# mLSTM chunk products in a hybrid backbone on one Trainium2 core: state products and scores alternate between partition halves

## The chip, the cores and the metric

The kernel runs on one core of a Trainium2 chip. Times are device microseconds of one launch, from the runs of the whole program. A core has TensorE (matmuls, with a loader of weights that overlaps them; PE and PEld in the profile), VectorE (DVE), ScalarE (ACT), GpSimd (POOL) and SyncE (SP, which here only issues DMAs). Matmul results go to PSUM, which the program uses in banks of 128 partitions by 512 fp32 values.

## The reference

A two-layer backbone over 256 context and 256 latent tokens of width 1024. Each layer is half a SwiGLU feed-forward, a token mixer, half a SwiGLU feed-forward. The mixer of layer 0 is a bidirectional mLSTM (8 heads, key width 64, value width 128, chunks of 128 tokens), that of layer 1 a retention. What matters here is one chunk of the mLSTM, for one head and direction:

```
s   = (q k^T) * exp(d - m_t)                          # 128 x 128, masked
num = w_inter * (q C) + s v                           # 128 x 128
den = w_inter * (q n) + sum(s)
h   = num / max(|den|, exp(-m_t))
C, n = w_prev * (C, n) + k^T (w_s * v), w_prev * n + k^T w_s
```

`C` is the state that the chunks before left (64 x 128), `n` its normaliser. The first context chunk of each direction has no state yet.

## The kernel before, in words

Everything lies on one core. Large matmuls are made from three products of split fp32r parts (`mm3`, lines 151 to 153), with weights streamed from memory, split by ScalarE and VectorE (lines 147 and 148) and used once. TensorE, ScalarE, VectorE and GpSimd each run their instructions in the order in which a scheduler, with its own simulated times, has put them; under `in_order()` TensorE's instructions keep the order in which they are written.

The mLSTM is done for two groups of four heads (`hh` 0 and 1). Of a group's four heads, two pairs `i` and in each pair `g` = 0 or 1: head `g` has its 64 key channels on partitions 0 to 63 or 64 to 127 of `q` and `k`. `ktok` transposes the keys, `states` computes the states of both directions for the chunks (line 738; its outputs alternate between partition halves), and `intra(s, hh)` computes the outputs of segment `s` (0 context, 1 latent), which has two chunks `c`, in two directions `d`. So there are four calls of `intra`, each with four chunks of four heads. `n` is a chunk's place in its direction; where `n` is 0 there is no state.

`intra` first makes the scores (line 761): for each half `g` one PSUM bank with four products of 64 x 128 by 64 x 128. For each direction it loads a broadcast of the row maxima (`E`, tile `b4`, L769, by GpSimd) and of the state weights (`WI`, L772), masks `E` (GpSimd, L776), takes exponentials (ScalarE, L779), multiplies them by the scores (VectorE, L782) and weights `q` (L783). Then for each chunk and each half `g` a bank gets, for the two pairs, `E` times the values (L794, contracting over 128 tokens) and `WI` times the state (L797, contracting over the half's 64 channels), the two taking turns in one accumulation. Column 128 is the denominator: ScalarE takes its magnitude (L800), VectorE bounds and inverts it (L801, L802), and the outputs are scaled into `hs` by ScalarE in direction 0 (L806) and added by VectorE in direction 1 (L808). `fin` normalises `hs` over the head, multiplies by the gate (GpSimd, L833) and transposes it (TensorE, L836) for the output projection.

All banks named `A` come from one pool of four; scores, chunk outputs and transposes share it. The calls stand among projections: the values and gates (`vo`, banks `Y`) beside the two calls of `hh` 0, then the states of `hh` 1, `intra(0, 1)`, the first output products, and `intra(1, 1)`, which is chained in written order with the next output products (`wout`).

Of the kernel before, what the change touches and what calls it, by code (L numbers as in the profile page):

```python
# [17 lines left out]
AF = mybir.ActivationFunctionType  # L18
# [69 lines left out]
def build(nc, tc, dr, out):  # L88
    V, S, G, TE = nc.vector, nc.scalar, nc.gpsimd, nc.tensor
# [15 lines left out]
    def bankA():  # L105
        return psA.tile([128, 512], F32, name="A", tag="A")
# [4 lines left out]
    def t2k(dtype=F32, n=512):  # L111
        return tmp.tile([128, 520], dtype, name="t", tag="t")[:, :n]

    def in_order():

        return tc.manual_schedule(engines={mybir.EngineType.PE})

    def seg(s):
        return slice(s * 256, s * 256 + 256)
# [345 lines left out]
    def mlstm(on_tile, on_seg):  # L465
# [138 lines left out]
        def chain(*f):  # L604

            def fn(W):
# [4 lines left out]
            return (fn,) + f[-1][1:]  # L611

        res += [part(ktok, 0), part(states, 0), part(intra, 0, 0)] + v1 + [part(intra, 1, 0)] + v2
        res += [part(ktok, 1)] + v3[:1] + [part(states, 1)] + v3[1:]
        res += [part(fin, 0, 0), part(intra, 0, 1), part(fin, 1, 0), wout(0, 0), chain(part(intra, 1, 1), wout(0, 1)), part(fin, 0, 1),
                part(fin, 1, 1), wout(1, 0), wout(1, 1)]
        res.append((lambda W: st.close(), None, None))
# [132 lines left out]
    def intra(X, s, hh):  # L750

        q, k, v = X["q"], X["k"], X["v"][hh]
        ti = [slice(s * 256 + c * 128, s * 256 + c * 128 + 128) for c in range(2)]
        sb = []
        for g in range(2):
            ps = bankA()
            o = g * 64
            for i in range(2):
                for c in range(2):
                    x = (i * 2 + c) * 128  # L760
                    TE.matmul(ps[:, x:x + 128], k[o:o + 64, hh * 2 + i, ti[c]], q[o:o + 64, hh * 2 + i, ti[c]],
                              start=True, stop=True)
            sb.append(ps.rearrange("p (i t) -> p i t", i=2))
        hs = X["p2"].tile([128, 2, 4, 128], F32, name="hs", tag="hs")
        X["hs"][s, hh] = hs
        for d in range(2):
            r0 = d * 32 + s * 16 + hh * 8
            E = X["p2"].tile([128, 8, 128], F32, name="b4", tag="b4")
            nc.gpsimd.dma_start(out=E, in_=X["nwd"][0][r0:r0 + 8].partition_broadcast(128))  # L769
            WI = t2k().rearrange("p (i t) -> p i t", i=2)  # L770
            for g in range(2):
                nc.gpsimd.dma_start(  # L772
                    out=WI[g * 64:g * 64 + 64],
                    in_=X["nwd"][1][r0:r0 + 8].rearrange("(i g c) t -> g i (c t)", g=2, c=2)[g].partition_broadcast(64))
            sg = 1 - 2 * d
            G.affine_select(out=E, in_=E, pattern=[[0, 8], [sg, 128]], base=0, channel_multiplier=-sg,  # L776
                            compare_op=ALU.is_ge, fill=NEG)
            for x in range(8):
                S.activation(out=E[:, x], in_=E[:, x], func=AF.Exp, bias=X["a"][:, r0 + x:r0 + x + 1])  # L779
            Ev = E.rearrange("p (i g c) t -> p g i (c t)", i=2, g=2)  # L780
            for g in range(2):
                V.scalar_tensor_tensor(out=Ev[:, g], in0=sb[g], scalar=0.125, in1=Ev[:, g], op0=ALU.mult, op1=ALU.mult)  # L782
            V.scalar_tensor_tensor(out=WI, in0=q[:, hh * 2:hh * 2 + 2, seg(s)], scalar=0.125, in1=WI,  # L783
                                   op0=ALU.mult, op1=ALU.mult)
            emv = X["em"][:, r0:r0 + 8].rearrange("p (i g c) -> p g c i", i=2, g=2)
            for c in range(2):
                n = s * 2 + (c ^ d)
                hv = hs[:, c].rearrange("p (i g) e -> p g i e", g=2)
                for g in range(2):
                    o = g * 64  # L790
                    ps = bankA()[:, :258].rearrange("p (i e) -> p i e", i=2)
                    with in_order():
                        for i in range(2):
                            TE.matmul(ps[:, i, :], E[:, i * 4 + g * 2 + c], v[:, s * 2 + c, 2 * i + g, :],  # L794
                                      start=True, stop=(n == 0))
                            if n:
                                TE.matmul(ps[:, i, :], WI[o:o + 64, i, c * 128:c * 128 + 128], X["C", d, n - 1][o:o + 64, i],  # L797
                                          start=False, stop=True)
                    dn = small.tile([128, 2], F32, name="dn")
                    S.activation(out=dn, in_=ps[:, :, 128], func=AF.Abs)  # L800
                    V.tensor_tensor(out=dn, in0=dn, in1=emv[:, g, c], op=ALU.max)  # L801
                    V.reciprocal(out=dn, in_=dn)  # L802
                    hg = hv[:, g]
                    for i in range(2):
                        if d == 0:
                            S.activation(out=hg[:, i, :], in_=ps[:, i, 0:128], func=AF.Copy, scale=dn[:, i:i + 1])  # L806
                        else:
                            V.scalar_tensor_tensor(out=hg[:, i, :], in0=ps[:, i, 0:128], scalar=dn[:, i:i + 1],  # L808
                                                   in1=hg[:, i, :], op0=ALU.mult, op1=ALU.add)

    def fin(X, s, hh):
# [498 lines left out]
    for i, (fn, src, mode) in enumerate(steps):  # L1310
# [3 lines left out]
        n = wi[i]  # L1314
# [14 lines left out]
```

## Time and profile before

| | |
|---|---|
| median of 3 runs | 1918.21 us (1915.36 to 1919.32) |
| the profiled execution | 1913.94 us, span 1912.1 us |
| TensorE busy | 1878.6 us (98%) |
| VectorE, ScalarE, GpSimd busy | 62%, 36%, 9% |
| DMA | 147 GB/s mean |
| mean granted TensorE clock | 0.991 |

The span runs from the first to the last instruction; the rest of the execution's time lies around it. The mLSTM's chunks are in 500 to 640 us of the span. The profile gives for each matmul a record with its start and a modelled end, so that neighbouring records overlap; how long an instruction holds the engine is read from the start of one to the start of the next. A product of two fp32 operands has two records. A form such as 64\*128 is the part of the array that an instruction uses: rows (the contraction) by columns. A release behind an arrow is what ended the idle time ahead of a row.

### The profile page before, as it was taken

What the parts mean: (1) busy time and instruction counts of PE and PEld (TensorE: products, weight loads), DVE (VectorE), ACT (ScalarE), POOL (GpSimd) and SP (SyncE); (2) the same over time, 40 slices, a digit from 0 to 9 for tenths busy, and PEclk for the clock granted to TensorE, in tenths of its full rate; (3) what the DMA queues carried; (4) which work ended last, traced back from release to release, by engine and by line L of the source; (5) the groups of instructions that cost most, each with busy time, mean ns of one, the idle gap of its engine ahead of it and who ended that gap; (6) DMA issues with size and microseconds to landing.
All of it is one profiled execution on the core that took longest, in us unless ns stands there. A gap on an engine that the chain in (4) does not pass through costs nothing.

```text
span 1912.1 us, 25440 instructions
## 1 busy us (share of the span) xinstructions
PE 1878.6 (98%) x10142; PEld 1617.0 (85%) x10142; DVE 1192.0 (62%) x1965; ACT 696.8 (36%) x1061; POOL 167.2 (9%) x207
## 2 busy tenths in 40 slices
PE   8999999999999999999999999999999999999998
PEld 6888888887777898888888988888898888889998
DVE  6858878566866566677764655555466555565554
ACT  4432232243553352222333422223244444444443
POOL 3000000110132210000001000000112120110001
PEclk9999999999998999999999999999999999989999
DMA  8536656223323234455542344554334244235652
GB/s 315 194 125 209 209 176 206 91 86 99 102 94 100 100 100 139 148 198 176 187 176 89 111 145 167 187 195 165 116 105 129 98 138 132 99 123 170 205 177 89
DMA packets 171689, 280.58 MB, mean 147 GB/s; under 512 B 6210, under 2 KB 108738, under 8 KB 171186
## 3 DMA queue, kind: packets, MB, share of 16 engines
q1 hardware_dynamic: 168656, 268.59, 42.0%
q0 software_dynamic: 2912, 10.36, 1.7%
q8 instruction: 80, 1.31, 0.3%
q14 instruction: 39, 0.31, 0.0%
q10 hardware_dynamic: 2, 0.01, 0.0%
HBM read 277.82 MB, written 1.11 MB: 146 GB/s over the span
## 4 chain that ended last, share of the span: by engine, by line
PE 91%; DVE 4%; ACT 2%; DMA 1%; issue 1%; POOL 1%; SPq 0%; POOLq 0%; DVEq 0%; ACTq 0%
PE A L152 18%; PE A L151 18%; PE A L153 18%; PE Y L152 11%; PE Y L151 11%; PE Y L153 11%; PE A L794 1%; PE A L797 1%; PE Y L1095 1%; DVE wl L148 1%; DMA XT<-xt 0%; DMA t<-nwd 0%; ACT wh L147 0%; DVE XT L210 0%; DVE so L551 0%
## 5 line engine op out<-in xcount | busy, mean ns | idle before, releaser
L148 DVE TENSOR_TENSOR wl<-raw,wh 128x1024 fp32r<-128x1024 f32 x360 | 448.0, 1245 | 465.9 <-ACT wh L147 465.6
L147 ACT ACTIVATE wh<-raw 128x1024 fp32r<-128x1024 f32 x360 | 382.2, 1062 | 808.1 <-PE A L152 324.7
L152 PE MATMUL A<-xl,wh 128*128 128x512 f32 (+1 forms) x1712 | 599.5, 352 | 6.8 <-DVE xl L148 6.1
L153 PE MATMUL A<-xh,wl 128*128 128x512 f32 (+1 forms) x1712 | 598.2, 351 | 0.0
L151 PE MATMUL A<-xh,wh 128*128 128x512 f32 (+1 forms) x1712 | 592.4, 352 | 5.6 <-ACT xh L1112 2.6
L152 PEld LDWEIGHTS A<-xl,wh 128*128 128x128 f32 x1712 | 325.8, 190 | 51.0 <-DVE xl L148 7.6
L151 PEld LDWEIGHTS A<-xh,wh 128*128 128x128 f32 x1712 | 321.5, 191 | 48.9 <-ACT xh L1112 2.9
L153 PEld LDWEIGHTS A<-xh,wl 128*128 128x128 f32 x1712 | 325.8, 190 | 42.4
L247 DVE CUSTOM_DVE_ANT_0 mj<-mr,mc,VT 128x1024 bf16<-128x1024 f32 x224 | 287.0, 1281 | 4.7 <-DMA mr<-mod_t 1.9
L153 PE MATMUL Y<-gh,wl 128*128 128x512 f32 (+1 forms) x704 | 246.0, 350 | 0.0
L151 PE MATMUL Y<-gh,wh 128*128 128x512 f32 (+1 forms) x704 | 245.5, 350 | 0.0
L152 PE MATMUL Y<-gl,wh 128*128 128x512 f32 (+1 forms) x704 | 245.3, 349 | 0.0
L153 PEld LDWEIGHTS Y<-gh,wl 128*128 128x128 f32 x704 | 132.3, 188 | 18.5
L152 PEld LDWEIGHTS Y<-gl,wh 128*128 128x128 f32 x704 | 132.4, 188 | 18.2
L151 PEld LDWEIGHTS Y<-gh,wh 128*128 128x128 f32 x704 | 132.3, 188 | 17.5
L152 PE MATMUL Y<-wl,xh 128*128 128x512 f32 x320 | 126.2, 395 | 0.0
L151 PE MATMUL Y<-wh,xh 128*128 128x512 f32 x320 | 125.3, 393 | 0.0
L153 PE MATMUL Y<-wh,xl 128*128 128x512 f32 x320 | 125.0, 392 | 0.0
L173 POOL TENSOR_TENSOR nacc<-nacc,nsq 128x256 f32<-128x256 f32 x50 | 41.6, 840 | 644.8 <-ACT nsq L169 643.4
L147 ACT ACTIVATE gh<-s 128x512 fp32r<-128x512 f32 (+1 forms) x88 | 48.7, 568 | 84.9 <-DVE s L338 84.9
L210 DVE SCALAR_TENSOR_TENSOR XT<-Y,GT,XT 128x256 f32<-128x256 f32 x148 | 63.8, 477 | 21.3 <-PE Y L153 21.1
L338 DVE TENSOR_TENSOR s<-s,A 128x512 f32<-128x512 f32 (+1 forms) x88 | 54.3, 619 | 28.5 <-PE A L153 28.2
(269 smaller groups left out, 1826.2 us busy)
## 6 DMA issues: line engine op xcount, KB each, us to landing
raw<-w SPq DMA_DIRECT2D x126, 1024.0 KB, 5.2
mr<-mod_t SPq DMA_DIRECT2D x128, 512.0 KB, 3.9
raw<-r_in SPq DMA_DIRECT2D x24, 1024.0 KB, 5.2
raw<-m_in SPq DMA_DIRECT2D x12, 1024.0 KB, 5.3
raw<-r_out SPq DMA_DIRECT2D x8, 1024.0 KB, 5.6
raw<-w SPq DMA_DIRECT2D x12, 512.0 KB, 3.7
w<-mod_t SPq DMA_DIRECT2D x8, 512.0 KB, 10.7
w<-mod_s SPq DMA_DIRECT2D x8, 512.0 KB, 10.6
```

The costliest lines, as they stand in the source:

```text
L147: S.activation(out=hi, in_=src, func=AF.Copy)
L148: return V.tensor_tensor(out=lo, in0=src, in1=hi.bitcast(F32), op=ALU.subtract)
L151: TE.matmul(ps, l[0], r[0], start=first, stop=False)
L152: TE.matmul(ps, l[0], r[1], start=False, stop=False)
L153: return TE.matmul(ps, l[1], r[0], start=False, stop=last)
L173: G.tensor_tensor(out=N[s][0], in0=N[s][0], in1=sq, op=ALU.add)
L210: V.scalar_tensor_tensor(out=XT[:, k, seg(s)], in0=ps, scalar=gate[:, s, k:k + 1], in1=XT[:, k, seg(s)], op0=ALU.mult, op1=ALU.add)
L247: V.tensor_tensor_reduce(out=mp["j"], in0=raw[i], in1=mp["c"][:, w], scale=1.0, scalar=MB[:, l * 72 + f:l * 72 + f + 1], op0=ALU.mult, op1 ...
L338: V.tensor_tensor(out=g[:, a:z], in0=sv[m][:, a:z], in1=ps[m][:, a:z], op=ALU.mult)
L794: TE.matmul(ps[:, i, :], E[:, i * 4 + g * 2 + c], v[:, s * 2 + c, 2 * i + g, :], start=True, stop=(n == 0))
L797: TE.matmul(ps[:, i, :], WI[o:o + 64, i, c * 128:c * 128 + 128], X["C", d, n - 1][o:o + 64, i], start=False, stop=True)
L1095: TE.matmul(ps, U["w", k][:, 0, c * 128:(c + 1) * 128], SC.rearrange("p (w k) -> p k w", w=2)[:, c], start=(c == 0), stop=(c == KT - 1))
```

## The change

The four score products of the two halves are written in alternation, half 0 then half 1, into two banks that are both taken first, and keep that order. A chunk takes both halves' banks at once; all eight products go out in written order: first the four with values, both halves one after the other, then the four with states, which alternate between the halves and so between the two banks. The first product of a bank starts it, the later ones accumulate into it. The arithmetic, the operands and the evacuation are the same, except that a half is read out after both banks are complete.

```diff
-        sb = []
-        for g in range(2):
-            ps = bankA()
-            o = g * 64
+        sb = [bankA() for _ in range(2)]
+        with in_order():
             for i in range(2):
                 for c in range(2):
-                    x = (i * 2 + c) * 128
-                    TE.matmul(ps[:, x:x + 128], k[o:o + 64, hh * 2 + i, ti[c]], q[o:o + 64, hh * 2 + i, ti[c]],
-                              start=True, stop=True)
-            sb.append(ps.rearrange("p (i t) -> p i t", i=2))
+                    for g in range(2):
+                        x, o = (i * 2 + c) * 128, g * 64
+                        TE.matmul(sb[g][:, x:x + 128], k[o:o + 64, hh * 2 + i, ti[c]], q[o:o + 64, hh * 2 + i, ti[c]],
+                                  start=True, stop=True)
+        sb = [ps.rearrange("p (i t) -> p i t", i=2) for ps in sb]
...
+                pb = [bankA()[:, :258].rearrange("p (i e) -> p i e", i=2) for _ in range(2)]
+                with in_order():
+                    for g in range(2):
+                        for i in range(2):
+                            TE.matmul(pb[g][:, i, :], E[:, i * 4 + g * 2 + c], v[:, s * 2 + c, 2 * i + g, :],
+                                      start=(i == 0 or n == 0), stop=(n == 0))
+                    for i in range(2 * (n > 0)):
+                        for g in range(2):
+                            o = g * 64
+                            TE.matmul(pb[g][:, i, :], WI[o:o + 64, i, c * 128:c * 128 + 128], X["C", d, n - 1][o:o + 64, i],
+                                      start=False, stop=(i == 1))
                 for g in range(2):
-                    o = g * 64
-                    ps = bankA()[:, :258].rearrange("p (i e) -> p i e", i=2)
-                    with in_order():
-                        for i in range(2):
-                            TE.matmul(ps[:, i, :], E[:, i * 4 + g * 2 + c], v[:, s * 2 + c, 2 * i + g, :],
-                                      start=True, stop=(n == 0))
-                            if n:
-                                TE.matmul(ps[:, i, :], WI[o:o + 64, i, c * 128:c * 128 + 128], X["C", d, n - 1][o:o + 64, i],
-                                          start=False, stop=True)
                     dn = small.tile([128, 2], F32, name="dn")
-                    S.activation(out=dn, in_=ps[:, :, 128], func=AF.Abs)
+                    S.activation(out=dn, in_=pb[g][:, :, 128], func=AF.Abs)
...
```

In the changed file the scores are line 760, the products with values line 792, those with states line 797, and most later lines move by one.

On TensorE, around the scores of `intra(1, 1)` (`q`, `k`), between the transposes of `fin` and the first output products, the order before is:

```order
L836 MATMUL A<-ident,hs 128x128 x8
L761 MATMUL A<-q,k 128x128 x4
L151 MATMUL Y<-xh,wh 128x512 x4
L761 MATMUL A<-q,k 128x128 x4
L152 MATMUL Y<-xl,wh 128x512
```

and after the change:

```order
L837 MATMUL A<-ident,hs 128x128 x8
L760 MATMUL A<-q,k 128x128 x8
L151 MATMUL Y<-xh,wh 128x512 x4
L152 MATMUL Y<-xl,wh 128x512
```

The two blocks of four scores have become one of eight, ahead of the output products.

On TensorE, the first chunk of `intra(1, 1)` in direction 0 (`b` with its number is the tile `E`, `v` the values, `C` the state, `t` the weighted queries) before:

```order
L794 MATMUL A<-v_3924,b_4882 128x129
L797 MATMUL A<-C_4432,t 128x129
L794 MATMUL A<-v_3924,b_4882 128x129
L797 MATMUL A<-C_4432,t 128x129
L794 MATMUL A<-v_3924,b_4882 128x129
L797 MATMUL A<-C_4432,t 128x129
L794 MATMUL A<-v_3924,b_4882 128x129
L797 MATMUL A<-C_4432,t 128x129
```

and after, all four chunks of the call:

```order
L792 MATMUL A<-v_3915,b_4858 128x129 x4
L797 MATMUL A<-C_4414,t 128x129 x4
L792 MATMUL A<-v_3915,b_4858 128x129 x4
L797 MATMUL A<-C_4438,t 128x129 x4
L792 MATMUL A<-v_3915,b_4927 128x129 x4
L797 MATMUL A<-C_4450,t 128x129 x4
L792 MATMUL A<-v_3915,b_4927 128x129 x4
L797 MATMUL A<-C_4426,t 128x129 x4
```

Where the two kinds took turns product by product, four of one kind now stand ahead of four of the other.

On GpSimd, between the last mask of `E` for `intra(0, 1)` and the broadcasts of `WI` for `hh` 1 (`ng` is the norm's gain, `so` the gate) before:

```order
L160 TENSOR_TENSOR rsb<-rsa,mhalf 128x8
L776 AFFINE_SELECT b_4674<-b_4674 128x1024
L833 TENSOR_TENSOR hs<-hs,so_4211 128x512 x3
L538 DMA ng<-m_ng 128x512
L833 TENSOR_TENSOR hs<-hs,so_4211 128x512
L540 TENSOR_SCALAR ng<-ng 128x512
L772 DMA t<-nwd_3297 64x2x256 x8
```

and after:

```order
L775 AFFINE_SELECT b_4653<-b_4653 128x1024
L834 TENSOR_TENSOR hs<-hs,so_4193 128x512 x2
L160 TENSOR_TENSOR rsb<-rsa,mhalf 128x8
L538 DMA ng<-m_ng 128x512
L540 TENSOR_SCALAR ng<-ng 128x512
L834 TENSOR_TENSOR hs<-hs,so_4193 128x512 x2
L771 DMA t<-nwd_3297 64x2x256 x8
```

The DMA of the gain and its scaling now stand ahead of two of the four multiplications with the gate, and the broadcasts of `WI` directly behind those two.

## Rows read from the trace of the kernel before

**Rows 1.** The page: TensorE's share, and the chain that ended last, by engine.

```profile
PE 1878.6 (98%) x10142; PEld 1617.0 (85%) x10142; DVE 1192.0 (62%) x1965; ACT 696.8 (36%) x1061; POOL 167.2 (9%) x207
...
PE 91%; DVE 4%; ACT 2%; DMA 1%; issue 1%; POOL 1%; SPq 0%; POOLq 0%; DVEq 0%; ACTq 0%
```

**Rows 2.** Stretches: us, then busy us of PE, PEld, DVE, ACT, POOL, clock, DMA.

```profile
500.00:560.00 60.00, 59.82 (x306) 46.45 (x305) 35.65 (x127) 26.27 (x73) 12.93 (x17) 1.00 0.31 106
590.00:613.00 23.00, 18.95 (x76) 14.43 (x74) 11.27 (x35) 6.50 (x22) 1.90 (x3) 0.63 0.21 70
626.70:640.10 13.40, 13.40 (x67) 9.46 (x65) 5.59 (x25) 4.55 (x16) 0.00 (x0) 1.00 0.25 79
```

**Rows 3.** TensorE's waits over the span: us in total, times, longest.

```profile
PE A L794 <- DVE b L782: 3.8, 2, 2.8
```

**Rows 4.** Timeline of TensorE in intra(0,0): start us, us, engine, line.

```profile
515.10 0.83 PE L794 MATMUL A<-v,b 128*128 128x129 f32 x6
515.86 0.49 PE L797 MATMUL A<-C,t 64*128 64x129 f32 x2
516.27 0.49 PE L794 MATMUL A<-v,b 128*128 128x129 f32 x2
```

**Rows 5.** Line 794: records, ns (min/median/max), first and last start.

```profile
L794 PE MATMUL A<-v,b x128: 271/275/582, 513.0 to 639.4; 128*128 128x129 f32 x128
```

**Rows 6.** Timeline of TensorE, start of intra(1,1) and what follows it.

```profile
626.80 0.38 PE L794 MATMUL A<-v,b 128*128 128x129 f32 x2
...
640.06 0.50 PE L151 MATMUL Y<-xh,wh 128*128 128x512 f32 x1
```

**Rows 7.** Timeline of TensorE: scores of intra(0,0), first half, and of intra(0,1).

```profile
503.24 1.16 PE L761 MATMUL A<-q,k 64*128 64x128 f32 x8 [0.18 <-DVE C L745]
504.32 0.50 PE L152 MATMUL Y<-wl,xh 128*128 128x512 f32 x1
...
590.32 1.71 PE L761 MATMUL A<-q,k 64*128 64x128 f32 x16
```

**Rows 8.** Line 761 alone, in short stretches of intra(0,1): PE, PEld, clock, DMA.

```profile
590.30:590.86 0.56, 0.54 (x4) 0.55 (x5) 1.00 0.00 0
590.86:591.30 0.44, 0.44 (x9) 0.44 (x8) 1.00 0.00 0
```

**Rows 9.** Timeline of TensorE: products of the state update, alternating column halves.

```profile
501.51 1.54 PE L738 MATMUL A<-v,t 128*64 128x129 f32 x24
```

**Rows 10.** Timeline of TensorE in intra(0,1) and after it.

```profile
598.14 0.80 PE L797 MATMUL A<-C,t 64*128 64x129 f32 x2
...
609.04 2.09 PE L794 MATMUL A<-v,b 128*128 128x129 f32 x8
610.92 1.87 PE L836 MATMUL A<-ident,hs 128*128 128x128 f32 x8
613.39 1.16 PE L761 MATMUL A<-q,k 64*128 64x128 f32 x8 [0.60 <-DVE xl L148]
```

**Rows 11.** Timelines of POOL, DVE and PE ahead of intra(0,1)'s first product.

```profile
576.25 4.79 POOL L772 DMA_DIRECT2D t<-nwd  x8
...
586.75 1.36 DVE L783 SCALAR_TENSOR_TENSOR t<-q,t 128x512 f32<-128x512 f32 x2 [2.34 <-DMA t<-nwd]
...
593.41 1.29 DVE L782 SCALAR_TENSOR_TENSOR b<-A,b 128x512 f32<-128x512 f32 x2
...
594.85 0.68 PE L794 MATMUL A<-v,b 128*128 128x129 f32 x4 [2.82 <-DVE b L782]
```

**Rows 12.** Timeline of ACT in intra(1,1): the read-out of a chunk.

```profile
630.14 0.17 ACT L800 ACTIVATE dn<-A 128x2 f32<-128x2 f32 x1 [1.50 <-PE A L797]
630.62 1.14 ACT L806 ACTIVATE hs<-A,dn 128x128 f32<-128x128 f32 x4 [0.30 <-DVE dn L802]
```

**Rows 13.** Timelines of POOL and PE at the end of the mLSTM's heads.

```profile
647.57 2.76 POOL L833 TENSOR_TENSOR hs<-hs,so 128x512 f32<-128x512 f32 x2 [2.67 <-ACT hs L828]
...
651.08 1.91 PE L836 MATMUL A<-ident,hs 128*128 128x128 f32 x16
```

More of the change, by code (lines that the diff above doesn't have):

```diff
@@ L805, in intra @@
                         if d == 0:
-                            S.activation(out=hg[:, i, :], in_=ps[:, i, 0:128], func=AF.Copy, scale=dn[:, i:i + 1])
+                            S.activation(out=hg[:, i, :], in_=pb[g][:, i, 0:128], func=AF.Copy, scale=dn[:, i:i + 1])
                         else:
-                            V.scalar_tensor_tensor(out=hg[:, i, :], in0=ps[:, i, 0:128], scalar=dn[:, i:i + 1],
+                            V.scalar_tensor_tensor(out=hg[:, i, :], in0=pb[g][:, i, 0:128], scalar=dn[:, i:i + 1],
                                                    in1=hg[:, i, :], op0=ALU.mult, op1=ALU.add)
```

## The prediction

> **What bounds the kernel now.** First the share of each engine on the page and the chain that ended last: TensorE is busy 1878.6 us of a span of 1912.1 us, and 91% of the chain is TensorE [rows 1]. So time taken from TensorE comes off the end, unless something else is late at that place. Second the table by stretches for the mLSTM [rows 2]: TensorE is full in 500 to 560 and in 626.7 to 640.1, and in 590 to 613 it is busy 18.95 of 23.00 us at a granted clock of 0.63, so there it both waits and runs part of the time at 1.2 instead of 2.4 GHz. Third the list of waits: the products with values (L794) waited 3.8 us in two waits, both for VectorE's masked scores (L782) [rows 3]. Otherwise the chunks are bound by TensorE's own instruction times, and these are what the change can move.
>
> Each fp32 product appears in the trace as two matmul records. There are 128 records of products with values, 96 of products with states (12 of the 16 chunks have a state) and 64 of scores.
>
> **What a switch of array shape costs.** The timeline in 515.10 to 516.27 [rows 4] shows a product with values (form 128\*128) and one with states (form 64\*128) taking turns. A pair of records holds the engine for 0.41 us (515.86 to 516.27). Six records of one form are busy 0.83 us and one lasts 0.27 us [rows 5], so (0.83 - 0.27) / 5 = 0.112 us a record in sequence. The last call, intra(1,1), is wholly of this kind: from 626.80 to 640.06 it issues 64 records in 13.26 us, 0.207 us a record [rows 6]. So a change of form costs about 2 x (0.207 - 0.112) = 0.19 us, eight times a chunk before the change and twice after it.
>
> **What two halves side by side give.** Eight score records on one half take 1.08 us to the next instruction (503.24 to 504.32) [rows 7]. At 590.32 both halves' records stood next to each other: 16 records are busy 1.71 us where two blocks of eight have 2 x 1.16 = 2.32 us, and the table of short stretches counts 4 records in the first 0.56 us and 9 in the next 0.44 us at the same clock [rows 8]. So different halves with different banks overlap. The column halves of the state update, which already alternate, show the full effect: 24 records busy 1.54 us, against 0.27 + 23 x 0.112 = 2.85 us in sequence [rows 9]. Bounds for the four-and-four state records of a chunk: one half alone is 1.08 - 4 x 0.112 = 0.63 us (all overlapped), and 1.08 us if nothing overlaps. A third bound, that a change of half costs what a change of form does, would make it 8 x 0.207 = 1.66 us. I take 0.63, because in rows 8 the second half began while the first still had records to go.
> The Trainium skill says otherwise ("TensorE: Matmul & The Clock Gate", Step-by-step: matmuls stay in program order and only weight loads are pulled ahead). In before's program all eight records of one half precede all eight of the other, and the counts of rows 8 don't fit strict order. By the rule only one record of each product could overlap its neighbour, and I estimate some 2 us less gain over the kernel.
>
> **The sum, against the profiled execution (1913.94 us, span 1912.1).**
> A chunk with state before: 16 x 0.207 = 3.31 us. After: the eight value records 0.76 + 2 x 0.112 = 0.98 (six take 515.10 to 515.86, rows 4), plus 0.10 for coming in from the other form, plus 0.63, together 1.71. Gain 1.60.
> Ten such chunks run at full clock (six in 500 to 560, four in 626.7 to 640.1): 16.0 us. Chunks without state stay as they are.
> Scores: intra(1,0) and intra(1,1) go from two blocks of 1.08 to one of 1.08; in intra(0,0) the scheduler leaves one product alone (0.41) before seven (1.08), gain 0.67; in intra(0,1) they end before a wait, gain 0. Together 2.8 us.
> intra(0,1) runs for the most part at half clock [rows 2, 10]. From 598.14 to 609.04 it alternates 30 records in 10.90 us. After: 16 state records in two blocks of 2 x 0.63, and 14 value records at 1.88 / 8 = 0.235 (609.04 to 610.92), 3.3, in all 5.8 us. Gain 5.0. The clock rose again only after the unswitched value records and the transposes, by the scores at 613.39. If it rises no earlier, some 3 us of the following output products run at half speed: -1.5 (ends 0 and -2.5, the 5.0 us halved). Net 3.5 us.
> The start of intra(0,1) is not TensorE's to set. VectorE works without an idle time from the landing of the broadcast (586.75) to the masked scores (593.41), and TensorE gets going at 594.85 [rows 11]. That broadcast is issued by POOL at 576.25, behind L540, and its DMA L538 was issued behind VectorE's L551. If this chain stays where it is, all gained before 590 turns into a longer wait there. But L551 needs the gate projection of TensorE, and the order of POOL now has L538 and L540 ahead of two of the L833 multiplications, so I expect the chain to move with TensorE and to gain 1 us beside (ends: -10 if it does not move, +3 if all waits at 594.85 go).
> Evacuation: a chunk's two banks now become full together, and four banks serve everything. A pair takes two magnitudes of 0.17 each, 0.30 of VectorE's division and 1.14 for four scalings, 1.8 us [rows 12]. In intra(1,1) the third chunk takes the banks of the first. The first is done at 1.6; its second bank is free at 3.4, its first two scalings sooner, at 2.9. The third chunk starts at 1.6 + 1.7 = 3.3 with the first bank and comes to the second 0.5 later. So a wait of 0 to 0.4 us, inside the last term below. In 500 to 560 I cost it at nothing, because projections stand between the two directions of a call; with that cover gone it costs up to 1.8 a chunk.
> The end of the mLSTM: after intra(1,1) the output products keep TensorE until 651.08, and the last L833 on POOL ends at 650.33 (647.57 + 2.76) [rows 13]: 0.75 us of slack for a chain that also starts at the end of the chunks. VectorE gets its two last chunks 1.7 us apart instead of 3.3, so part of this slack goes; with the small waits above -1.0 us. From 654 on everything moves up unchanged, since TensorE is busy 98% of the whole span [rows 1].
> Sum: 16.0 + 2.8 + 3.5 + 1.0 - 1.0 = 22.3, say 22 us: 1913.94 - 22 = 1892 us for a profiled execution. The median of the runs, 1918.21, is 4.3 us above the profiled one, so 1918.2 - 22 = 1896 us.
>
> **Rivals.**
> 1. No useful overlap of the halves. Twelve state blocks at 1.08 instead of 0.63 lose 5.4, the scores their 2.8: gain 14, 1904 us. Against it: rows 8 and 9. For it: rows 8 are a single place with some 0.3 us saved (16 records in sequence would be busy 0.27 + 15 x 0.112 + 0.1 = 2.05, not 1.71). 8%.
> 2. The POOL and VectorE chain before 594.85 does not move. The 9.6 us of six chunks and 1.75 of scores vanish in the wait: gain 11, 1907 us. For it: VectorE has no gap in 586.75 to 593.41. Against: its start is tied to TensorE's projections. 12%.
> 3. The clock falls in intra(1,1) too, because its chunks now have gaps. Its 7 us become 14 and the gain there is gone: 1903 us. For it: the clock fell in 590 to 613 after the waits [rows 2, 11]. Against: expected gaps are below 0.5 us and the products before are dense. The Trainium skill's clock gate section ("TensorE: Matmul & The Clock Gate", Part 1) has half speed as the default that only activity lifts; this trace agrees with 0.63 there and 1.00 in the full stretches. 5%.
> 4. Slower. Every chunk waits for the evacuation of a pair before it, because two of four banks hold scores until both directions have read them, and a pair is only given back whole. Price: 16 x 1.8 = 29 us against the 22 gained, 1925 us. It decides from 22 / 16 = 1.4 us of wait a chunk. For it: before, one bank was filled while the other was read, and TensorE needed 8 x 0.207 = 1.66 us for a bank. Against: TensorE's order shows ten or more other products between the two directions of a call in 500 to 560. 4%.
> That the order isn't what it says is no rival: the rows of the order show four and four.
>
> **How the numbers follow.** Forecast 71%, rivals 8, 12, 5 and 4%. About 0.2% (3.8 us) is what a measurement here can tell from no change. Faster by more: the forecast and rivals 1 to 3, less a little for two of them together, 92%. Within: 4%. Slower: 4%. The range for 8 in 10: high end 1908, which takes in rivals 1 to 3; low end 1888, if the clock term is 0, the wait at 594.85 goes and the small waits do not come: 16 + 2.8 + 5 + 3 = 27, and 3 more for the spread of the runs (1915.36 to 1919.32).
>
> **What would show it.** In the profile after: value records in runs of eight or more 0.11 us apart; state records in pairs that start within some ns, a block of eight in about 0.65 us; intra(1,1) some 7 us long instead of 13.26; TensorE in 500 to 560 without new waits; intra(0,1) 5 us shorter at the same low clock; later stages equal in length. Wrong would be: waits of the value products for ScalarE (bank), a wait at the start of intra(0,1) above 5 us, a state block of 1.08 us, or a clock below 1.00 in intra(1,1).

## The result, and the profile after

The changed kernel takes 1892.22 us (median of 4 runs, 1891.5 to 1894.3) against 1916.78 us for the kernel before (4 runs, 1914.24 to 1919.32). The ratio is 0.9885, with a 95% interval of 0.9866 to 0.9904. The profiled execution took 1892.63 us with a span of 1890.9 us, which is 21.2 us less than the 1912.1 us of before.

The page of the changed kernel, TensorE's share and the chain that ended last, beside [rows 1]:

```profile
PE 1853.8 (98%) x10142; PEld 1601.9 (85%) x10142; DVE 1188.3 (63%) x1965; ACT 695.4 (37%) x1061; POOL 168.5 (9%) x207
...
PE 89%; DVE 4%; ACT 2%; issue 2%; POOL 1%; DMA 1%; POOLq 0%; DVEq 0%; ACTq 0%
```

As many matmul records as before, 24.8 us less busy time in a span that is 21.2 us shorter. So the gain is TensorE's own instruction time, nothing was left out, and TensorE's waits have grown by 3.6 us.

Where it comes from, by the starts of the same instructions in the two traces. A head here is one of the two groups of four (`hh` 0 is the first):

| Place | before, us | after, us | ahead by | gained since the row above |
|---|---|---|---|---|
| first score product (L761, L760) | 503.24 | 503.48 | -0.24 | -0.24 |
| L716, after both intra calls of the first head | 562.87 | 551.49 | 11.38 | 11.62 |
| first value product of intra(0,1) | 594.85 | 585.31 | 9.54 | -1.84 |
| transposes after intra(0,1) | 610.92 | 594.26 | 16.66 | 7.12 |
| first value product of intra(1,1) | 626.80 | 613.17 | 13.63 | -3.03 |
| first product after intra(1,1) (L151) | 640.06 | 620.01 | 20.05 | 6.42 |
| L151 after the last transposes | 654.11 | 634.06 | 20.05 | 0 |
| end of the span | 1912.1 | 1890.9 | 21.2 | 1.15 |

The rows of the second place and of the last transposes, before (L716, L151) and after (L716, its first five records):

```profile
562.87 1.03 PE L716 MATMUL A<-ident,k 128*128 128x128 f32 x8
654.11 0.36 PE L151 MATMUL A<-xh,wh 128*128 128x256 f32 x1 [1.12 <-ACT xh L147]
```

```profile
551.49 0.71 PE L716 MATMUL A<-ident,k 128*128 128x128 f32 x5
```

The three kinds of block that the change makes, first in the first head (answers to [rows 4] and [rows 7]); the timeline of TensorE has start us, us, engine, line:

```profile
515.09 1.50 PE L792 MATMUL A<-v,b 128*128 128x129 f32 x12
516.53 0.71 PE L797 MATMUL A<-C,t 64*128 64x129 f32 x8
...
529.39 1.16 PE L760 MATMUL A<-q,k 64*128 64x128 f32 x16
```

Sixteen score records are busy 1.16 us, as long as eight were in [rows 7] and less than the 1.71 us of sixteen there. Eight state records are busy 0.71 us. To the next instruction they hold TensorE for 0.65 us. Line 797 alone, in two short stretches at the start of this block (PE, PEld, clock, DMA), beside [rows 8]:

```profile
516.50:516.60 0.10, 0.07 (x2) 0.08 (x2) 1.00 0.00 0
...
516.80:517.30 0.50, 0.44 (x8) 0.25 (x6) 1.00 0.00 0
```

Two records are under way in the first 0.07 us, where records of one half stand 0.11 us and more apart: the halves start as pairs. The whole call intra(1,1), beside [rows 6]:

```profile
613.17 1.05 PE L792 MATMUL A<-v,b 128*128 128x129 f32 x8
614.15 0.71 PE L797 MATMUL A<-C,t 64*128 64x129 f32 x8
614.80 1.16 PE L792 MATMUL A<-v,b 128*128 128x129 f32 x8
...
619.36 0.71 PE L797 MATMUL A<-C,t 64*128 64x129 f32 x8
620.01 0.50 PE L151 MATMUL Y<-xh,wh 128*128 128x512 f32 x1
```

It takes 6.84 us instead of 13.26, no wait inside: 1.71 us a chunk.

The stretch between the two, beside [rows 7], [rows 10] and [rows 11], is where gains came and went:

```profile
578.94 1.16 PE L760 MATMUL A<-q,k 64*128 64x128 f32 x16
585.31 1.23 PE L792 MATMUL A<-v,b 128*128 128x129 f32 x4 [5.21 <-DVE b L781]
587.10 2.95 PE L792 MATMUL A<-v,b 128*128 128x129 f32 x12 [0.56 <-DVE b L781]
589.98 0.74 PE L797 MATMUL A<-C,t 64*128 64x129 f32 x8
590.66 1.16 PE L792 MATMUL A<-v,b 128*128 128x129 f32 x8
...
594.26 1.14 PE L837 MATMUL A<-ident,hs 128*128 128x128 f32 x8 [0.71 <-DVE hs L809]
597.03 0.76 PE L760 MATMUL A<-q,k 64*128 64x128 f32 x2 [1.62 <-DVE hs L809]
598.77 2.07 PE L760 MATMUL A<-q,k 64*128 64x128 f32 x14 [0.98 <-DVE xl L148]
```

The wait for the masked scores grew from 2.82 to 5.21 us. The clock, which was low (1.2 GHz) until about 612.6 before, is full (2.4 GHz) again from about 590: at 590.66 eight value records take 1.16 us. Then it falls a second time, which the 2.07 us of the scores at 598.77 show. Over the two low pieces and the full one between them (columns as in [rows 2]) it is 0.67:

```profile
583.20:603.70 20.50, 14.52 (x79) 12.06 (x80) 14.41 (x53) 9.22 (x34) 4.95 (x5) 0.67 0.32 104
```

The waits of 0.71, 1.62 and 0.98 us behind the call are for PSUM banks. The transposes at 594.26 read only `hs` of the first head, which POOL finished at 568.31 (its rows below), and the scores read only `q` and `k`. What VectorE's L809 and L148 give back there is the bank that they read: that of the last chunk, then that of the transposes.

Ahead of the 5.21 us wait stand POOL and VectorE. POOL first, before (what stands ahead of [rows 11]) and after:

```profile
568.76 0.62 POOL L538 DMA_DIRECT2D ng<-m_ng  x1 [0.98 <-DVE so L551]
569.41 1.34 POOL L833 TENSOR_TENSOR hs<-hs,so 128x512 f32<-128x512 f32 x1
573.99 2.29 POOL L540 TENSOR_SCALAR ng<-ng 128x512 f32<-128x512 f32 x1 [3.24 <-DMA ng<-m_ng]
```

```profile
557.87 0.62 POOL L538 DMA_DIRECT2D ng<-m_ng  x1
563.33 1.50 POOL L540 TENSOR_SCALAR ng<-ng 128x512 f32<-128x512 f32 x1 [4.83 <-DMA ng<-m_ng]
564.82 3.49 POOL L834 TENSOR_TENSOR hs<-hs,so 128x512 f32<-128x512 f32 x2
568.25 4.77 POOL L771 DMA_DIRECT2D t<-nwd  x8
```

and VectorE, from the landing of that broadcast to the masked scores:

```profile
575.11 0.69 DVE L782 SCALAR_TENSOR_TENSOR t<-q,t 128x512 f32<-128x512 f32 x1 [3.48 <-DMA t<-nwd]
...
580.31 2.49 DVE L551 SCALAR_TENSOR_TENSOR so<-so,ng 128x512 f32<-128x512 f32 x4
...
584.57 1.28 DVE L781 SCALAR_TENSOR_TENSOR b<-A,b 128x512 f32<-128x512 f32 x2
```

POOL stood 4.83 us waiting for the gain's DMA, 3.24 before. From the issue of that DMA to the first broadcast it takes 10.4 us (557.87 to 568.25), 7.5 before (568.76 to 576.25). So its broadcasts are issued 8.0 us earlier than in [rows 11], while TensorE had come 11.4 us ahead. VectorE then worked without a gap from 575.11 on.

### The profile page after: what moved, and what is told of

It is laid out like the page before. It is cut to its first block, busy times and chain, and to the rows that moved or that the text cites. A ratio compares the mean times of both kernels' runs of the same rounds, so it can differ in the third digit from the quotient of the medians.

```text
span 1890.9 us, 25444 instructions
## 1 busy us (share of the span) xinstructions
PE 1853.8 (98%) x10142; PEld 1601.9 (85%) x10142; DVE 1188.3 (63%) x1965; ACT 695.4 (37%) x1061; POOL 168.5 (9%) x207
## 4 chain that ended last, share of the span: by engine, by line
PE 89%; DVE 4%; ACT 2%; issue 2%; POOL 1%; DMA 1%; POOLq 0%; DVEq 0%; ACTq 0%
PE A L152 18%; PE A L153 18%; PE A L151 18%; PE Y L151 11%; PE Y L152 11%; PE Y L153 11%; DVE wl L148 1%; PE A L792 1%; DMA b<-nwd 1%; PE Y L1096 1%; DVE XT L210 0%; DVE xl L148 0%; DMA t<-nwd 0%; POOL hs L834 0%; DVE mj L1100 0%
## 5 line engine op out<-in xcount | busy, mean ns | idle before, releaser
L148 DVE TENSOR_TENSOR wl<-raw,wh 128x1024 fp32r<-128x1024 f32 x360 | 448.8, 1247 | 472.1 <-ACT wh L147 471.7
L151 PE MATMUL A<-xh,wh 128*128 128x512 f32 (+1 forms) x1712 | 593.3, 352 | 5.7 <-ACT xh L1113 2.6
L151 PEld LDWEIGHTS A<-xh,wh 128*128 128x128 f32 x1712 | 321.9, 191 | 49.2 <-ACT xh L1113 2.9
L151 PE MATMUL Y<-gh,wh 128*128 128x512 f32 (+1 forms) x704 | 245.5, 350 | 0.0
L151 PEld LDWEIGHTS Y<-gh,wh 128*128 128x128 f32 x704 | 132.3, 188 | 17.6
L151 PE MATMUL Y<-wh,xh 128*128 128x512 f32 x320 | 125.2, 393 | 0.0
```

Source lines behind the costliest of these rows:

```text
L148: return V.tensor_tensor(out=lo, in0=src, in1=hi.bitcast(F32), op=ALU.subtract)
L151: TE.matmul(ps, l[0], r[0], start=first, stop=False)
```

## The experiments

In the experiments the kernel before was run again beside the kernels tried, with medians of 1913.42 (19 runs), 1912.99 (17) and 1914.05 us (7). Each ratio below is against the runs beside it. They put the gain of the change nearer to the 21 us of the spans than to the 24.6 us between the two medians above.

**The chunks alone.** The changed kernel with the scores of before, half by half and with no kept order:

```diff
-        sb = [bankA() for _ in range(2)]
-        with in_order():
+        sb = []
+        for g in range(2):
+            ps = bankA()
...
```

Expected: 

> The chunks as in the changed kernel (four value products, then four state products in alternating halves and banks), the scores as before (one half's bank after the other). Theory A (the gain is the chunks' and the scores add a little): state blocks of 0.65 us, intra(1,1) 6.8 us; the scores' 2.8 us are missing, of which those of intra(1,0) may come back if both halves stand next to each other anyway: 1893 to 1896 us, 21 to 24 us under before. Rival B (the scores' order carries a good part, since it also moves the masked scores and POOL's chain): 1900 us or more.

Measured: 1892.69 us (1891.74 to 1895.11), ratio 0.9893 (0.9875 to 0.9912). The scores of intra(1,0) in its timeline:

```profile
530.10 1.71 PE L761 MATMUL A<-q,k 64*128 64x128 f32 x16
```

As long as in [rows 7], against 1.16 us after the change. Yet the time is that of the changed kernel within the spread, and a little below theory A's range. The first value product of intra(0,1) comes at 584.78 after a wait of 2.44 us instead of 585.31 after 5.21: TensorE comes to it later and starts earlier. So what the scores gain ahead of that wait ends in it. The run doesn't price the scores by themselves, since the scheduler gave POOL another order here: two of the multiplications stand between the issue of the gain's DMA and its use, POOL waits 0.61 us for that DMA, and the broadcasts go out at 567.25, 1.0 us earlier than in the changed kernel.

**The scores alone.** The kernel before with the changed kernel's scores (the same lines the other way round).

Expected: 

> Only the scores alternate; in the chunks values and states take turns bank by bank as before. Theory A: 16 score records of both halves in about 1.1 us instead of twice 1.08, gain up to 2.8 us: 1913 to 1916 us. Rival B (scores carry a good part): 1908 us or less.

Measured: 1911.72 us (1908.93 to 1914.31, 12 runs), ratio 0.9988 (0.9978 to 0.9998), so some 1.7 us. The block of sixteen and the first value product behind it:

```profile
590.27 1.16 PE L760 MATMUL A<-q,k 64*128 64x128 f32 x16
594.86 1.23 PE L793 MATMUL A<-v,b 128*128 128x129 f32 x4 [3.43 <-DVE b L781]
```

The value product starts where it did before (594.85), with a longer wait (3.43 for 2.82 us): what the scores of intra(0,1) gain is lost in it. Those of the first head are not lost. This profile came 1.4 us later to the first score product (504.61 for 503.24) and has made that up at 590.27. In the medians the gain of 1.7 us is below theory A's 2.8, with 0.4 to 4.2 us open.

**State products half by half.** The changed kernel with the four state products of a chunk written two and two:

```diff
-                    for i in range(2 * (n > 0)):
-                        for g in range(2):
+                    for g in range(2 * (n > 0)):
+                        for i in range(2):
```

Expected: 

> The changed kernel with the four state products of a chunk written half by half (first half's two, then the other's two) instead of alternating; banks and all else the same. Theory A (each half of the array takes its own instructions, and starts the next half's as soon as they are in the queue): state blocks stay at about 0.65 us, time equal to the changed kernel, 1892 us. Rival B (matmuls start in the order of the program, so only neighbours of different halves overlap): state blocks of 0.9 to 1.1 us, twelve of them, 3 to 5 us more: 1895 to 1897 us.

Measured: 1893.05 us (1892.57 to 1893.46), ratio 0.9892 (0.9876 to 0.9907). A state block in its timeline, and line 797 alone in the first 0.1 us of another:

```profile
617.35 0.72 PE L797 MATMUL A<-C,t 64*128 64x129 f32 x8
```

```profile
517.55:517.65 0.10, 0.06 (x2) 0.06 (x2) 1.00 0.00 0
```

The block is as short as with alternation (0.72 against 0.71 us busy), as theory A had it. In the second block shown, the second record starts 14 ns after the first (517.592 and 517.606). The trace doesn't name the half; but records of one half stand 0.11 us and more apart, so the second is one of the other half, although three records of the first half stand ahead of it in the written order, which `in_order()` keeps. The order of starts is not the program's, and alternation is not what gives the overlap.

**Half the switches, no halves side by side.** The kernel before with two value products, then two state products in each bank:

```diff
                         for i in range(2):
                             TE.matmul(ps[:, i, :], E[...], v[...],
-                                      start=True, stop=(n == 0))
-                            if n:
-                                TE.matmul(ps[:, i, :], WI[...], X["C", d, n - 1][...],
-                                          start=False, stop=True)
+                                      start=(i == 0 or n == 0), stop=(n == 0))
+                        for i in range(2 * (n > 0)):
+                            TE.matmul(ps[:, i, :], WI[...], X["C", d, n - 1][...],
+                                      start=False, stop=(i == 1))
```

Expected: 

> Before's kernel with one edit: in each bank the two value products come first, then the two state products, so a chunk changes form four times instead of eight, no state products of different halves stand next to each other, and a bank is still read out by itself. Scores as before. Theory A (a change of form costs 0.19 us, and that is the larger part): a chunk with state falls from 3.31 to 16 x 0.112 + 4 x 0.19 = 2.55 us, 0.76 x 10 = 7.6 us at full clock and 2 to 3 us in intra(0,1): 1906 to 1909 us. Rival B (the gain of the change is overlap, switches cost little by themselves): 1914 us or more.

Measured: 1904.44 us (1900.5 to 1909.61, 8 runs), ratio 0.9955 (0.994 to 0.9969), 9.0 us less than before. intra(1,1) in its timeline, first and last rows, and the stretch from intra(0,1) to the scores of intra(1,1):

```profile
623.42 0.61 PE L794 MATMUL A<-v,b 128*128 128x129 f32 x4
623.96 0.71 PE L797 MATMUL A<-C,t 64*128 64x129 f32 x4
624.60 0.71 PE L794 MATMUL A<-v,b 128*128 128x129 f32 x4
...
632.93 0.71 PE L797 MATMUL A<-C,t 64*128 64x129 f32 x4
```

```profile
589.00:616.30 27.30, 25.84 (x88) 20.87 (x87) 13.45 (x56) 11.30 (x38) 6.32 (x7) 0.50 0.21 72
```

The call takes 10.15 us (623.42 to 633.57), 2.54 a chunk. With 0.112 us a record and 0.19 us a change of form that is 16 x 0.112 + 4 x 0.19 = 2.55. So the price of a change holds at four a chunk as it does at eight. That it is the change of form, and not two products in a row in one accumulation, is read from the rows around [rows 4]: a pair of records with states and the next pair with values hold TensorE for the same time (515.86 to 516.27 to 516.69, 0.41 and 0.42 us), though only the step from values to states stays in one accumulation. The changed kernel has two changes, 16 x 0.112 + 2 x 0.19 = 2.17, and measures 1.71; the 0.46 between them is what the halves side by side save (a block of eight in sequence 1.08, measured 0.65). Of the 1.60 us a chunk, some 1.15 are switches and 0.45 the overlap. The median is below theory A's 1906 to 1909 us and far from rival B's 1914. The clock stayed low for 27.3 us here, longer than in either kernel; one profile shows it, and the runs spread over 9 us.

**The gain loaded once.** To test what sets the start of intra(0,1): the changed kernel with the gain `ng` loaded and halved once, at the start of the mLSTM, so that L538, its DMA and L540 go from POOL's queue there.

```diff
+            X["ng"] = p.tile([128, 1024], F32, name="ng")
+            nc.gpsimd.dma_start(out=X["ng"], in_=dr["m_ng"].to_broadcast([128, 1024]))
+            G.tensor_scalar(out=X["ng"], in0=X["ng"], scalar1=0.5, scalar2=None, op0=ALU.mult)
...
-                            ng = X["p"].tile([128, 512], F32, name="ng", tag="ng")
...
```

Expected: 

> The changed kernel with one more edit: the gain ng of m_norm_g is loaded and halved once at the start of the mLSTM (both heads' halves), so POOL no longer issues L538, waits 4.83 us for that DMA and runs L540 (1.50 us) between the two pairs of output multiplications before it issues the eight broadcasts for intra(0,1). Theory C: the wait of 5.21 us before the second chunk's... first value product of intra(0,1) is the end of this chain: without some 6.9 us (0.62 + 4.83 + 1.50) POOL issues the broadcasts at about 561 to 562 instead of 568.25, and VectorE (whose work before the masked scores then becomes the limit: back to back from 575.11 to about 585) starts earlier by what DMA and its own projections allow; the wait falls to 0 to 2.5 us, the clock does not fall there, and the kernel is 3 to 7 us faster than the changed one, 1885 to 1889. Theory D: VectorE's own work (the adds and multiplications between 575 and 585) or ScalarE's exponentials set the start and POOL was only late beside them: wait unchanged within 1 us, time within 1.5 us of the changed kernel.

Measured: 1892.38 us (1889.82 to 1894.6), ratio 0.9887 (0.9868 to 0.9906): no different from the changed kernel. Its timelines of POOL, of VectorE, of TensorE and of ScalarE:

```profile
564.27 4.79 POOL L770 DMA_DIRECT2D t<-nwd  x8 [0.16 <-issue]
```

```profile
574.17 1.40 DVE L781 SCALAR_TENSOR_TENSOR t<-q,t 128x512 f32<-128x512 f32 x2 [1.59 <-DMA t<-nwd]
...
581.48 1.28 DVE L780 SCALAR_TENSOR_TENSOR b<-A,b 128x512 f32<-128x512 f32 x2
```

```profile
582.22 1.23 PE L791 MATMUL A<-v,b 128*128 128x129 f32 x4 [2.64 <-DVE b L780]
...
596.04 2.07 PE L151 MATMUL Y<-xh,wh 128*128 128x512 f32 x4 [2.94 <-ACT xh L147]
```

```profile
592.47 2.44 ACT L777 ACTIVATE b<-b,a 128x128 f32<-128x128 f32 x8 [2.05 <-POOL b L774]
...
594.93 1.06 ACT L147 ACTIVATE xh<-A 128x512 fp32r<-128x512 f32 x2
```

The first step is theory C's: without the DMA the broadcasts go out 4.0 us earlier, and the wait falls from 5.21 to 2.64 us. The time is theory D's. POOL doesn't reach the 561 to 562 of the expectation: its last multiplication ends at 564.12, and a buffer for the broadcasts comes free only with TensorE's products of the state update. The first broadcast starts 0.14 us after the 24th record of these (564.14). The clock fell here too, and inside the call it stayed low until 588.5. Behind the chunks a wait of 2.94 us for ScalarE's xh, which had eight exponentials of the next call ahead of it (2.44 us), stands in place of the 1.62 and 0.98 us of the changed kernel. So the expectation failed in POOL's step and in those behind the wait. Of the 3.1 us by which the call starts earlier, 0.5 were there before the first head; 2.3 are left at the transposes behind the call, 2.0 in the profiled span (1888.9 us), and nothing that can be told in the medians.

**The same edit in the kernel before.** Expected: 

> The kernel before with the same one edit (the gain loaded and halved once). In before the first product waited 2.82 us and the clock was low in 595.5 to 612.6. Theory C: that wait is mostly the POOL chain as well, so it goes or falls below 1 us, and the low clock shortens or goes: 2 to 8 us faster than before, 1906 to 1911 by the runs' median of 1913. Theory D: the wait stays, within 1.5 us of before. If both kernels gain the same, the edit is independent of the change; if the changed kernel gains more, the change had turned part of its gain into this wait.

Measured: 1914.35 us (1912.03 to 1920.14, 12 runs), ratio 1.0007 (0.9993 to 1.002): nothing. Its timelines of POOL and TensorE:

```profile
578.18 4.79 POOL L771 DMA_DIRECT2D t<-nwd  x8 [5.43 <-PE A L737]
```

```profile
596.73 1.20 PE L793 MATMUL A<-v,b 128*128 128x129 f32 x4 [2.70 <-DVE b L781]
```

Without L540 the broadcasts wait 5.43 us for TensorE's products of the state update (L737, in the kernels without this edit L738), again until 0.14 us after their 24th record (578.05), and go out no earlier than in [rows 11]; this profile is 2.0 us late from before the first head on. In the kernel before the 24th record starts at 576.04, so these products alone would have held the broadcasts until 576.2, and the gain's DMA cost nothing. In the changed kernel it starts at 564.66, and the broadcasts came 3.5 us later than that allows: the faster TensorE, with POOL's new order, uncovered the DMA.

**Scores in pairs.** The changed kernel with two score products on one half, then two on the other (the loops over `c` and `g` exchanged).

Expected: 

> The changed kernel with its scores issued as two products on one half, then two on the other, and so on (before: four and four; changed: one and one). It tests how far ahead the records of the other half are taken. Theory Q (the other half's first record starts once no more than three records of the first half are still to start, as in the blocks of sixteen where it began beside the fifth of eight records, and in the states half by half where it began 14 ns after the first of four): a block of sixteen takes about 1.09 us, as in the changed kernel (1.09). Rival (only a direct neighbour overlaps, half of each pair runs alone): about 1.3 to 1.6 us. Time of the kernel within 1 us of the changed one either way.

Measured: 1892.09 us, one run. The block of sixteen:

```profile
527.59 1.26 PE L760 MATMUL A<-q,k 64*128 64x128 f32 x16
```

The time can't be told from the changed kernel's. 1.26 us busy: 0.10 more than alternating (1.16), 0.45 less than four and four (1.71). To the next instruction it holds TensorE for 1.19 us, between the 1.09 of theory Q and the 1.3 of the rival's lower end. So the other half is taken ahead by some records, not without limit, and "no more than three" is near but not the whole rule; its exact form stays open.

**The gate off VectorE.** The run with the gain loaded once, and for the second head (so + 1) times ng on POOL:

```diff
-                                V.scalar_tensor_tensor(out=so, in0=so, scalar=1.0, ...)
+                                    G.tensor_scalar(out=so, in0=so, scalar1=1.0, scalar2=None, op0=ALU.add)
+                                    G.tensor_tensor(out=so, in0=so, in1=ngu, op=ALU.mult)
```

Expected: 

> The changed kernel with the gain loaded once (as in the run before) and the second head's gate combination (so + 1) times ng taken from VectorE (L551, four of 0.68 us, 2.49 us as a group, ahead of the masked scores of intra(0,1)) and given to POOL as two instructions each. In the run with the gain loaded once VectorE worked from 574.17 to 581.48 without a gap before the first masked scores, 2.49 us of it these four. Theory V: VectorE's queue is now what the first value product of intra(0,1) waits for; it starts about 2.5 us earlier (579.7 instead of 582.22, right behind the scores that end at 579.5), its wait falls from 2.64 us to 0 to 0.5. But the start of the output products after this call is set by the last chunk's read-out, its transposes and ScalarE's xh behind eight exponentials (waits of 0.79 and 2.94 us), and these move only with the chunks: if they move along, 2 to 2.5 us less than with the gain alone (1889.9 by the medians); if ScalarE's exponentials (which wait for POOL's selects of the next call, now behind some 13 us of gate work) stay where they are or come later, the wait there grows by as much and the time is unchanged within 1 us. I take the second as likelier. Theory W (ScalarE or a DMA sets the start): the wait of 2.64 us stays within 0.5.

Measured: 1890.1 us (1888.57 to 1892.31, 4 runs), ratio 0.9882 (0.9863 to 0.9902). Its timelines of VectorE and TensorE:

```profile
578.37 1.64 DVE L148 TENSOR_TENSOR wl<-raw,wh 128x1024 fp32r<-128x1024 f32 x1 [1.60 <-ACT wh L147]
```

```profile
581.38 0.77 PE L795 MATMUL A<-v,b 128*128 128x129 f32 x4 [2.66 <-DVE b L784]
...
595.01 1.63 PE L151 MATMUL Y<-xh,wh 128*128 128x512 f32 x4 [2.60 <-ACT xh L147]
```

The wait stays (2.66 for 2.64 us), so theory V falls and W holds: the 2.49 us taken off VectorE are filled by a wait of 1.60 us for ScalarE's `wh`, which stands ahead of the masked scores in VectorE's queue, and by that split's longer run. Its median is 2.1 us below the changed kernel's and the ranges overlap; whether it is faster is not settled, nor what its lead would come from, since both waits are still there. That the median is theory V's 1889.9 us is no sign for V, whose wait did not fall.

## Why the prediction was right

It came out at 1892.22 us where 1896 was forecast; for the profiled execution it said 1892 and 1892.63 was measured. The gain of 21.2 us in the spans stands against a sum of 22.3. What TensorE does at full clock came as forecast; the other terms missed by -2.8, -0.5, +1.0 and +1.15 us and in part cancel, so that the sum is as near as 1.1 us is luck. By its steps:

- **A change of form costs 0.19 us.** Right. Eight, four and two changes a chunk gave 3.31, 2.54 and 1.71 us, each as 16 x 0.112 plus the changes, less 0.46 for the overlap in the last. The price comes from the first and the overlap from the last, so the second is the test.
- **Two halves side by side: 0.63 us a block of eight.** Right, 0.65. The block of 1.08 of rival 1 does not occur. The Trainium skill ("TensorE: Matmul & The Clock Gate", Step-by-step) keeps matmuls in program order. The half-by-half run contradicts that for the order of starts: a record that stands fifth in the program started second.
- **Sixteen us at full clock, with the scores' 2.8.** In the first head 9.6 + 1.75 = 11.35 expected, 11.62 measured. In intra(1,1) 6.4 expected, 6.42 measured, at a full clock, so rival 3 did not come. But the scores' share did not last: those of the first head end in the wait before intra(0,1), which with POOL's other order is why the kernel with the old scores is as fast; those of intra(1,1) ran at half clock behind two waits. Alone the scores gave 1.7 us.
- **The start of intra(0,1): +1.0 expected, -1.84 measured.** This is the term with the wrong sign, within its ends of -10 and +3, and its wait passed the 5 us named as a mark of being wrong. The chain did move with TensorE, but by 8.0 us at POOL and not 11.4. The order showed L540 ahead of two multiplications, and the prediction took that for a gain. It was a loss: with no multiplication inside it any more, POOL's wait at L540 for the DMA grew from 3.24 to 4.83 us, and the two multiplications (3.49 us) now stand between it and the broadcasts. The run with the gain loaded once took 2.6 us off TensorE's wait, so this chain is part of it. It is not all of it. In this stretch SyncE loads 1 MB of weights (`raw<-m_out`), and broadcasts that are issued behind that load land only about when it does. Before, the first broadcast was issued at 576.25, ahead of the load (577.73), and landed after 2.9 us; now all eight are issued behind it (568.25 against 567.20), and the first lands after 6.3 us, at 574.53, the load at 574.21. With the scores in pairs they went out 1.4 us earlier (566.88, the load 565.83) and landed no earlier (574.80), and TensorE waited 6.40 us. With the gain loaded once three of the eight went ahead of the load, and only those landed early. All ten profiles agree with this, but no run moves the load, so it is read and not tested.
- **intra(0,1): 5.0 less 1.5 expected, 7.12 less 3.03 measured.** The assumed clock was wrong in both halves: it rose inside the call, not after it, and fell again behind it. The stretch of the 3.03 also holds the scores of intra(1,1), which were to gain 1.08 us; with them 4.6 was expected in all and 4.1 measured, near by errors that cancel. The waits behind the call grew from 0.60 us [rows 10] to 3.31 (0.71 + 1.62 + 0.98). They are for banks: the last chunk is read out while TensorE has nothing else, and its two banks and those of the transposes are what the next products need.
- **Tail and small waits: -1.0 expected, 0 measured.** The row that answers to the wait after [rows 13]:

```profile
634.06 0.36 PE L151 MATMUL A<-xh,wh 128*128 128x256 f32 x1 [1.12 <-ACT xh L147]
```

It comes 20.05 us earlier, exactly as much as the end of intra(1,1), so the slack of 0.75 us was enough. No wait for a bank appears in the chunks, so rival 4 did not come there; its mechanism is what made the waits behind intra(0,1), at 3.31 us and not 29.
- **Unchanged from 654 on.** Nearly: 1.15 us more came where a piece of low clock near the end is shorter (6.8 us from 1685.8 on, 10.2 from 1704.9 on before). One profile each shows it, and no cause was tested.

The median was forecast 4 us too high because the runs shown of before lay above its profiled execution, and those of after do not.

## What to carry to other kernels

Count how often TensorE changes its form and price it from two neighbouring rows: 0.19 us a change here, more than a whole fp32 record of 0.112. Group products of one form, and put the row halves of a pair next to each other in different banks; with two products a half strict alternation is not needed. Then look at what the faster stretch runs into: what is gained ahead of a latency chain (a broadcast behind a DMA, a read-out that holds banks) can be lost there, 1.84 of 11.38 us here, and clearing one such wait only showed the next. Look, too, at the order of the other engines' queues after the change: an order that looks better can lengthen a chain.

## What the runs showed of the hardware that was not expected

- Records of the other row half start ahead of records of the first half that precede them in the program: 14 ns after the first record when two products of each half stand together (block 0.65 us to the next instruction). In blocks of four products a half the overlap is partial (1.71 us busy for sixteen), in pairs nearly full (1.26), alternating full (1.16).
- The low clock is not a fixed loss. After the 2.82 us wait of [rows 11] it lasted until 612.6; after the longer wait of 5.21 us it was full again inside the call, and fell a second time; with half the switches it stayed at 0.50 for 27.3 us, with TensorE busy 25.84 of them. The profile of before did not give a size for it.
- A small DMA issued behind a large load can land with it: 2.9 us to landing for the broadcasts of 128 KB ahead of the load of 1 MB before, 6.3 us for the first one behind it in the changed kernel (read from the traces, not tested).
